# A layout of its own for the edge blocks of a windowed attention

## The chip, the cores and the metric

The kernel runs on one core of one Trainium2 chip. The metric is the device time of one execution in microseconds. The engines of the core are TensorE (PE in the profile; its weight loads are PEld), VectorE (DVE), ScalarE (ACT), GpSimd (POOL) and SyncE (SP, which here only issues DMAs). Each engine runs its own instructions in order and waits for the others by semaphores.

## What is computed

The reference is one layer of an encoder block. An input of 256 tokens and one of 2048 tokens, each with 16 learned meta tokens put ahead, are normalized and projected (1024 to 2304 columns). The columns feed two groups: a windowed attention of 8 query heads over 2 key heads, and a convolution of width 31. Both are gated, concatenated, projected back and added to the input. The part that the change is about, cut from the reference:

```python
qb = qr.reshape(B, nb, BLOCK, N_KV_HEADS, GQA_GROUP, hd)      # blocks of 128 queries
kw = jnp.concatenate([kp[:, :-2], kp[:, 1:-1], kp[:, 2:]], axis=2)   # left, own, right block of keys
valid = (jnp.abs(rel) <= WINDOW)[None] & in_range[:, None, :]
s_win = jnp.einsum('bnqkgd,bnskd->bnkgqs', qb, kw) * scale - (slopes * dist)
s_win = jnp.where(valid, s_win, -jnp.inf)
s_meta = jnp.einsum('bnqkgd,bmkd->bnkgqm', qb, km) * scale
p = softmax(concatenate([sink_b, s_meta, s_win]))
o = p_meta @ vm + p_win @ vw
```

A query sees the 16 meta keys, and the real keys at most 128 away. A sequence's first block has no left neighbour and its last block no right one.

## The kernel before

**Stages.** The input projections run first, over 18 blocks of 128 tokens in six groups of three, as three passes of products of high and low parts (each operand is split into a rounded part and its remainder). Queries, keys, values and gates go through DRAM. The convolution runs on VectorE beside the projections. During the last q projections the attention begins (`spread`, `attention_open`), and `attention_rest` runs the rest of it together with the output projection.

**Blocks and layout.** Blocks 0 and 1 are the short sequence, 2 to 17 the long one: 0 and 2 are first blocks, 1 and 17 last ones, and block 1 is followed by block 2. For each block and key head (`kv`) the scores of four query heads are made in four steps `n` of 32 queries x 4 heads = 128 rows. The key tile `kw` (two of them in turn) has 416 columns: half of the left block (`LA`), the meta keys (`MA`), the own block (`CC`), the other half of the left block (`LB`), half of the right block (`RA`), the meta keys again (`MB`), and the other half of the right block (`RB`). So each step reads one stretch of columns (`SPANS`, L62) that holds its window and the meta keys once. `span` (L312) cuts it for edge blocks; what lies in it and is not the block's (`masked`, L320) is filled with 1e30 on VectorE (L437).

**From scores to output.** `scores` (L410) issues two matmuls into a PSUM tile S (L427 in the code; the profile puts them on the wrapper's line L383), then `bias_max` (bias and row minimum, VectorE), `expo` (ScalarE) and, after the fourth step, `norm` (the reciprocal on VectorE and four products on GpSimd, L466). `bank` (L481) transposes the normalized rows in three groups: `c` the own block, `m` the columns `LB` to `MB`, `x` the meta keys with the outer half of a neighbour. Each group is four transposes into one PSUM tile, then split into high and low (`ptiles`). `pv` (L508) multiplies with the values: one matmul of 512 columns for each of high and low in `c` and `m` (L517), and in `x` two halves of 256 columns (L523), as two of the four steps need the left neighbour and two the right one. The rows of these products are 128 in `c`, 128 or 64 in `m`, 80 or 16 in `x`, with 64 and 16 where a neighbour is missing. `merge` (L532) adds the two parts, multiplies with the gate on GpSimd (L550) and splits the result for the output projection (`rest`, L554, L555).

**Order.** `slot_step` (L614) is one slot, eight to a block: one `bank` of the block before (`PLAN`, L475), two pieces of the output projection (L598, three matmuls each), one `scores` of the present block, loads, and `tick`. `later(k, f)` runs `f` at the k-th tick from there. On GpSimd the order is the program's during the attention, and from `attention_rest` on TensorE's too; for the other engines a planner sets the order from a simulated time line. The output projection of a block starts at slot 6 of the next step with the convolution's half (e = 4 to 7), and needs the attention's half (`rest`) four slots later for key head 0 and six later for key head 1.

**Loads.** `load_k` (L285) and `load_v` (L296) issue up to five and seven DMAs for a block, fewer for an edge block. `kw` holds its meta keys all the time; `km`, their source, is loaded in the middle of the projections (L1148).

Of the kernel before, what the change touches and what calls it, by code (L numbers as in the profile page):

```python
# [18 lines left out]
P = 128  # L19
# [39 lines left out]
SW = 2 * P + NM + QB  # L59
# [3 lines left out]
BOFF = (0, SW, 2 * SW, 3 * SW, 4 * SW + QB)  # L63
# [23 lines left out]
def hymba_kernel(  # L87
# [29 lines left out]
    vec = const.tile([P, 26], F32, name="vec")  # L117
# [4 lines left out]
    snk, nsnk = vec[:, 22:24], vec[:, 24:26]  # L122
# [114 lines left out]
    vt, qt, q2t, sbt, gat, gct, cnt, mix, att, yot, opj = ({} for _ in range(11))  # L237
# [3 lines left out]
    def attention_open():  # L241

        phase[0] = 2
        right_pools.close()
        man = ExitStack()
        cst['man'] = man
        man.enter_context(tc.manual_schedule(engines=MAN1))
        ap = att_pools.enter_context(tc.tile_pool(name="ap", bufs=2, side="right", reuse_waits="tile"))
        pool["a"] = ap
        cst["bias"] = bias = ap.tile([P, KV, BOFF[4]], BF16, tag="bias", name="bias", bufs=1)  # L250
        load_q(0)
        for i in range(2):
            kw.append(ap.tile([P, 2, KV, KW], F32R, tag=f"kw{i}", name=f"kw{i}", bufs=1))
        load_k(0)
        nc.sync.dma_start(bias, bias_c)
        for t, c0 in zip(kw, (LB, RA)):
            for at in (MA, MB):
                nc.gpsimd.tensor_copy(t[:, :, :, at : at + NM], km)
            nc.gpsimd.memset(t[:, :, :, c0 : c0 + QC].bitcast(F32), 0.0)
        for i in range(3):  # L260
            t = ap.tile([P, 4, KW], F32, tag=f"sb{i}", name=f"sb{i}", bufs=1)
            for n, c0 in enumerate((RA + QB, LA, RB + QB)):
                nc.vector.memset(t[:, n, c0 : c0 + QB], 0.0)
            sbs.append(t)
        load_v(0)
# [11 lines left out]
    def has_left(b):  # L277
        return b not in (0, NB_P)

    def has_right(b):  # L280
        return b not in (NB_P - 1, NB - 1)

    vt, qt, q2t, sbt, gat, gct, cnt, mix, att, yot, opj = ({} for _ in range(11))

    def load_k(b):  # L285
        t = kw[b % 2].bitcast(F32)
        at = P * (b - 1)
        nc.sync.dma_start(t[:, :, :, CC:LB], kd[:, :, :, at + P : at + 2 * P])
        if has_left(b):
            nc.sync.dma_start(t[:, :, :, LA:MA], kd[:, :, :, at : at + QC])  # L290
            nc.sync.dma_start(t[:, :, :, LB:RA], kd[:, :, :, at + QC : at + P])
        if has_right(b):
            nc.sync.dma_start(t[:, :, :, RA:MB], kd[:, :, :, at + 2 * P : at + 2 * P + QC])
            nc.sync.dma_start(t[:, :, :, RB:KW], kd[:, :, :, at + 2 * P + QC : at + 3 * P])

    def load_v(b):  # L296
        vt[b] = [
            pool["a"].tile([P, KV, P], F32R, tag=f"v{k}", name=f"v{k}_{b}", bufs=VBUFS) for k in ("c", "m", "a", "b")
        ]
        c, m, a, z_ = (t.rearrange("p a e -> p (a e)").bitcast(F32) for t in vt[b])  # L300
        nc.sync.dma_start(c, vd[b])
        r = QC if has_left(b) else 0
        if has_left(b):
            nc.sync.dma_start(m[0:QC], vd[b - 1, QC:P])
            nc.sync.dma_start(a[0:QC], vd[b - 1, 0:QC])
        nc.sync.dma_start(a[r : r + NM], vmd)
        nc.sync.dma_start(z_[0:NM], vmd)
        if has_right(b):
            nc.sync.dma_start(m[r : r + QC], vd[b + 1, 0:QC])
            nc.sync.dma_start(z_[NM:XR], vd[b + 1, QC:P])  # L310

    def span(b, n):  # L312
        c0, c1 = SPANS[n]
        if not has_left(b):
            c0 = max(c0, MA)
        if not has_right(b):
            c1 = min(c1, RA if n < 2 else RB)
        return c0, c1

    def masked(b, n):  # L320
        if not has_left(b):
            return LB
        if n >= 2 and not has_right(b):
            return RA
        return None
# [84 lines left out]
    def scores(b, kv, n):  # L410

        c0, c1 = span(b, n)
# [21 lines left out]
        def bias_max():  # L434
            off = masked(b, n)
            if off is not None:
                nc.vector.memset(ps[:, off - c0 : off - c0 + QC], BIG)  # L437
            nc.vector.tensor_tensor_reduce(  # L438
                out=sb[:, n, c0:c1],
                in0=ps[:, 0:w],  # L440
                in1=cst["bias"][:, kv, BOFF[n] + c0 - SPANS[n][0] : BOFF[n] + c1 - SPANS[n][0]],
                scale=1.0,
                scalar=nsnk[:, kv : kv + 1],
                op0=ALU.add,
                op1=ALU.min,
                accum_out=nm[:, n : n + 1],
            )
# [13 lines left out]
        def norm():  # L461
            nc.vector.tensor_tensor(es, es, rs, op=ALU.add)
            nc.vector.reciprocal(es, es)  # L463
            for k in range(4):
                a0, a1 = span(b, k)
                nc.gpsimd.tensor_scalar(  # L466
                    sb[:, k, a0:a1], sb[:, k, a0:a1], es[:, k : k + 1], 1.0, op0=ALU.mult, op1=ALU.mult
                )
# [9 lines left out]
    def edges(b):  # L478
        return (XR if has_left(b) else NM, XR if has_right(b) else NM)

    def bank(b, k, kv):  # L481
        pt = psum.tile([P, 4, P], F32, tag="b", name=f"pT{b}_{k}_{kv}")
        sb = sbt[b, kv]
        rows = [P] * 4
        for n in range(4):
            if k == "c":
                src = sb[:, n, CC:LB]
            elif k == "m":
                src = sb[:, n, LB if has_left(b) else RA : MB if has_right(b) else RA]
                rows[n] = src.shape[-1]  # L490
            else:
                r = rows[n] = edges(b)[n // 2]
                src = sb[:, n, MB : MB + r] if n >= 2 else sb[:, n, CC - r : CC]
            nc.tensor.transpose(pt[: rows[n], n, :], src, ident)  # L494

        def split():
            ph, pl = (pt_part(2 * (n_bank[0] % 4) + i) for i in range(2))
            n_bank[0] += 1
            halves = ((0, 4, rows[0]),) if rows[0] == rows[3] else ((0, 2, rows[0]), (2, 4, rows[3]))
            for n0, n1, r in halves:  # L500
                nc.scalar.copy(ph[:r, n0:n1], pt[:r, n0:n1])
                nc.vector.tensor_tensor(pl[:r, n0:n1], pt[:r, n0:n1], ph[:r, n0:n1], op=ALU.subtract)
            pv_st[b, k, kv] = (ph, pl)

        later(1, split)
        later(2, lambda: pv(b, k, kv))

    def pv(b, k, kv):  # L508
        parts = pv_st[b, k, kv]
        tc_, tm, ta, tb = vt[b]  # L510
        if k == "c":
            opj[b, kv] = psum.tile([P, 4, P], F32, tag="c", name=f"O{b}_{kv}")
        o = opj[b, kv]
        if k != "x":
            r = P if k == "c" or (has_left(b) and has_right(b)) else QC
            for i, t in enumerate(parts):
                nc.tensor.matmul(  # L517
                    o, (tc_ if k == "c" else tm)[:r, kv, :], t[:r], start=(k == "c" and i == 0), stop=False
                )
            return  # L520
        for h, (t, r) in enumerate(zip((ta, tb), edges(b))):
            for i, p in enumerate(parts):
                nc.tensor.matmul(  # L523
                    o[:, 2 * h : 2 * h + 2],
                    t[:r, kv, :],
                    p[:r, 2 * h : 2 * h + 2],
                    start=False,
                    stop=(h == 1 and i == 1),
                )
        later(1, lambda: merge(b, kv))  # L530
# [159 lines left out]
    if True:  # L690
# [424 lines left out]
        nc.sync.dma_start(vec[:, 0:24], vecs)  # L1115
# [128 lines left out]
def layout(inputs):  # L1244
# [27 lines left out]
    bias_c = np.zeros((P, KV, BOFF[4]), np.float32)  # L1272
    for kv in range(KV):
        for n in range(4):
            col = np.arange(*SPANS[n])
            seg = np.searchsorted([MA, CC, LB, RA, MB, RB], col, side="right")
            key = col - np.array([P, 0, CC, RA, RA - P, 0, RA - P + NM])[seg]
            meta = (seg == 1) | (seg == 5)
            dist = np.abs(key[None, :] - (QB * n + row % QB)[:, None]).astype(np.float32)
            full = np.where(dist <= P, slopes[4 * kv + local][:, None] * dist, np.float32(BIG))  # L1280
            bias_c[:, kv, BOFF[n] : BOFF[n + 1]] = np.where(meta[None, :], np.float32(0.0), full)
    w_out = f["w_out"][0].reshape(8, P, D)
    vecs = np.concatenate([vecs, sink], axis=1)
# [20 lines left out]
```

## Time and profile before

| | |
|---|---|
| time, median of 3 (range) | 957.39 us (957.22 to 957.50) |
| the profiled execution | 957.63 us |
| its span in the profile | 955.9 us |
| VectorE busy, instructions | 757.8 us (79%), 1295 |
| ScalarE busy, instructions | 429.0 us (45%), 1168 |
| GpSimd busy, instructions | 286.8 us (30%), 450 |
| DMA, read and written | 111.77 and 62.70 MB |

The span runs from the first to the last recorded instruction. The prediction below shows lines of several views. In the chain of waits in order of time a line is the start, the time until the next piece starts, the engine, the tile written, the line of the code, and how many instructions are merged. In the groups by line and shape it is: line, engine, operation, tile written and tiles read, sizes (rows*columns of the weights and partitions x elements streamed, for TensorE), the number, then total busy us and mean ns of one, then the idle time just before them and who ended it. The windows give busy time for each engine, then TensorE's granted clock, the DMA share and GB/s. The attention's slots begin at 578 us of the span, `attention_rest` at about 608, and the last block's values are multiplied at 926 to 944.

### The profile page before, as it was taken

To read this page: it belongs to the slowest core of one execution; us is meant where nothing else is said; L and a number is where in the kernel's file an instruction comes from. 1 tells how busy PE (TensorE), PEld (TensorE's weight loads), DVE (VectorE), ACT (ScalarE), POOL (GpSimd) and SP (SyncE) were. 2 spreads that over 40 slices of the span, in tenths; PEclk is the share of its full clock that TensorE was granted. 3 is DMA by queue.
4 is the path that set the end of the run, shared out by engine and by line. 5 is a ranking of instruction groups with operands and counts; after the bars stand their busy time and mean duration, and the time that the engine had idled before them with its cause. 6 is when DMAs were issued, how large, how long until landed. Compare 5 with 4: busy or idle time off the path is not lost.

```text
span 955.9 us, 16841 instructions
## 1 busy us (share of the span) xinstructions
PE 949.3 (99%) x5861; PEld 893.3 (93%) x5861; DVE 757.8 (79%) x1295; ACT 429.0 (45%) x1168; POOL 286.8 (30%) x450
## 2 busy tenths in 40 slices
PE   8999999999999999999999999999999999999998
PEld 8999999999999999999999999878888888888886
DVE  5579999997977789999995656777877677767763
ACT  7432111353458740011112456655666666656651
POOL 4310000283479300000001455443433242424240
PEclk9999999999999999999999999999999999999999
DMA  8585345784656593233334688965666566655411
GB/s 306 163 263 200 132 174 182 251 297 168 202 169 194 195 318 133 89 121 130 138 134 144 184 269 286 349 175 145 185 195 170 153 176 187 180 153 168 142 60 66
DMA packets 152948, 175.58 MB, mean 184 GB/s; under 512 B 44992, under 2 KB 115472, under 8 KB 152864
## 3 DMA queue, kind: packets, MB, share of 16 engines
q1 hardware_dynamic: 152864, 174.51, 56.3%
q8 instruction: 46, 0.75, 0.3%
q14 instruction: 38, 0.31, 0.1%
HBM read 111.77 MB, written 62.70 MB: 183 GB/s over the span
## 4 chain that ended last, share of the span: by engine, by line
PE 95%; DVE 2%; DMA 1%; issue 1%; POOL 0%; ACT 0%; SPq 0%; DVEq 0%; ACTq 0%
PE pj L852 42%; PE y L598 21%; PE pj L868 14%; PE S L383 4%; PE O L517 4%; PE O L523 2%; PE pT_c L494 2%; PE pT_x L494 2%; PE pT_m L494 2%; PE qT L383 1%; PE lnt L207 1%; PE lnu L226 1%; DVE y L935 1%; DMA kd<-ks 1%; DMA xn<-in_z 0%
## 5 line engine op out<-in xcount | busy, mean ns | idle before, releaser
L852 PE MATMUL pj<-xh,ws 128*128 128x384 f32 (+1 forms) x1536 | 395.9, 338 | 0.1
L935 DVE SCALAR_TENSOR_TENSOR y<-us,cw,y 128x1167 f32<-128x1167 f32 x240 | 329.3, 1438 | 0.4
L852 PEld LDWEIGHTS pj<-xh,ws 128*128 128x128 f32 x1536 | 280.1, 188 | 0.4 <-ACT xh L1105 0.4
L852 PE MATMUL pj<-xl,ws 128*128 128x384 f32 (+1 forms) x768 | 260.8, 340 | 0.1
L598 PE MATMUL y<-wo,rest 128*128 128x512 f32 (+1 forms) x672 | 173.4, 395 | 0.0
L868 PE MATMUL pj<-ws,xh 128*128 128x256 f32 (+1 forms) x880 | 165.8, 284 | 0.4 <-DVE qs L999 0.2
L852 PEld LDWEIGHTS pj<-xl,ws 128*128 128x128 f32 x768 | 144.1, 188 | 0.5 <-DVE xl L790 0.4
L598 PEld LDWEIGHTS y<-wo,rest 128*128 128x128 f32 x672 | 117.0, 189 | 22.5 <-issue 1.8
L868 PEld LDWEIGHTS pj<-ws,xh 128*128 128x128 f32 (+1 forms) x880 | 136.6, 187 | 1.4 <-issue 0.4
L868 PE MATMUL pj<-ws,xl 128*128 128x256 f32 (+1 forms) x440 | 124.1, 282 | 0.0
L450 ACT ACTIVATE sb<-sb,nm 128x304 f32<-128x304 f32 (+3 forms) x144 | 79.2, 550 | 48.2 <-DVE nm L438 47.6
L438 DVE CUSTOM_DVE_ANT_0 sb<-S,bias,vec 128x304 f32<-128x304 f32 (+3 forms) x144 | 76.2, 529 | 28.9 <-PE S L383 26.1
L960 ACT ACTIVATE go<-pj 128x384 f32<-128x384 f32 x48 | 23.5, 490 | 151.3 <-PE pj L852 138.7
L550 POOL TENSOR_TENSOR at<-at,ga 128x256 f32<-128x256 f32 x36 | 26.4, 735 | 201.8 <-DVE at L544 130.8
L466 POOL TENSOR_SCALAR sb<-sb,es 128x304 f32<-128x304 f32 (+3 forms) x144 | 75.9, 544 | 26.5 <-DVE es L463 20.6
L868 PEld LDWEIGHTS pj<-ws,xl 128*128 128x128 f32 (+1 forms) x440 | 82.2, 187 | 0.2
L134 POOL TENSOR_SCALAR ssk<-ssk 128x2 f32<-128x2 f32 x18 | 7.5, 419 | 213.2 <-ACT sqk L974 211.2
L383 PE MATMUL S<-kw,q 128*128 128x304 f32 (+3 forms) x288 | 64.1, 304 | 0.0
L383 PEld LDWEIGHTS S<-kw,q 128*128 128x128 f32 x288 | 53.1, 188 | 11.0 <-issue 0.2
L134 POOL TENSOR_SCALAR ssq<-ssq 128x4 f32<-128x4 f32 (+2 forms) x55 | 26.7, 485 | 92.8 <-ACT xn L715 74.1
L895 ACT ACTIVATE sg<-pj 128x384 f32<-128x384 f32 (+1 forms) x24 | 11.8, 493 | 82.6 <-PE pj L852 73.8
L598 PE MATMUL y<-wo,mch 128*128 128x512 f32 x144 | 47.3, 410 | 0.0
(134 smaller groups left out, 1325.9 us busy)
## 6 DMA issues: line engine op xcount, KB each, us to landing
wd<-ws SPq DMA_DIRECT2D x36, 512.0 KB, 6.1
ws<-wd SPq DMA_DIRECT2D x36, 512.0 KB, 5.7
wraw<-in_w_in SPq DMA_DIRECT2D x52, 256.0 KB, 6.4
xn<-in_z SPq DMA_DIRECT2D x18, 512.0 KB, 5.5
gd<-go SPq DMA_DIRECT2D x48, 192.0 KB, 2.1
yo<-in_z SPq DMA_DIRECT2D x36, 256.0 KB, 3.2
out_y<-yo SPq DMA_DIRECT2D x35, 256.0 KB, 2.4
kw<-kd SPq DMA_DIRECT2D x64, 128.0 KB, 3.8
```

Of the source, the lines that this page charges most:

```text
L134: nc.gpsimd.tensor_scalar(src, src, scale, eps, op0=ALU.mult, op1=ALU.add)
L383: r = f(*a, **k)
L438: nc.vector.tensor_tensor_reduce(out=sb[:, n, c0:c1], in0=ps[:, 0:w], in1=cst["bias"][:, kv, BOFF[n] + c0 - SPANS[n][0] : BOFF[n] + c1 - S ...
L450: nc.scalar.activation(sb[:, n, c0:c1], sb[:, n, c0:c1], AF.Exp, bias=nm[:, n : n + 1], scale=-1.0, accum_out=rs[:, n : n + 1],)
L466: nc.gpsimd.tensor_scalar(sb[:, k, a0:a1], sb[:, k, a0:a1], es[:, k : k + 1], 1.0, op0=ALU.mult, op1=ALU.mult)
L494: nc.tensor.transpose(pt[: rows[n], n, :], src, ident)
L517: nc.tensor.matmul(o, (tc_ if k == "c" else tm)[:r, kv, :], t[:r], start=(k == "c" and i == 0), stop=False)
L550: nc.gpsimd.tensor_tensor(at[:, pr, :], at[:, pr, :], gat[b][:, pr, :], op=ALU.mult)
L598: nc.tensor.matmul(ps, mh[mi][:, e % 4, :], wo[e, wi][:, cols], start=(e == 4 and k == 0), stop=(e == 3 and k == 2),)
L852: nc.tensor.matmul(ps[:, :n], ws[:, d, wi, P * half_i : P * half_i + P], x[xi][:, d, o : o + n], start=(k == 0), stop=(k == 3 * ND - 1),)
L868: nc.tensor.matmul(ps[:rows, :UW], x[xi][:, d, o : o + rows], ws[:, d, wi, :], start=(k == 0), stop=(k == 3 * ND - 1),)
L935: nc.vector.scalar_tensor_tensor(y[:, yo + o0 : yo + o1], u[:, o0 + k : o1 + k], cw[:, j, k : k + 1], y[:, yo + o0 : yo + o1], op0=ALU.mul ...
```

## The change

First and last blocks get a layout in which two full key blocks lie side by side: columns `CC` to `MB` hold 256 keys loaded by one DMA, with the meta keys ahead of them (first) or behind them (last). Spans hold only keys that the block has, so the fill with 1e30 goes, and the bias table gets rows for each kind. Columns of the score tile that a narrower span leaves are filled with zeros on GpSimd, as the transposes read them. The products with values take two full tiles of 128 keys in `c` and `m`.

The meta keys' part is taken apart: `norm` writes the 16 normalized meta columns of the four steps twice into a tile `pm` (128 x 128, one buffer), which one transpose turns. ScalarE copies it rounded, VectorE puts the remainder in the lower half of the rows, GpSimd spreads it by a 0/1 mask `msk` over 512 columns (`ph`), and one matmul multiplies it with `vm`, the meta values eight times over (loaded once by eight DMAs). This product comes three ticks after its transpose instead of two. Inner blocks are computed as before.

```diff
-SPANS = ((LA, RA + QB), (LA + QB, MB), (CC, RB + QB), (CC, KW))
+SPANS = {
+    "in": ((LA, RA + QB), (LA + QB, MB), (CC, RB + QB), (CC, KW)),
+    "first": tuple((MA, LB + QB * (n + 1)) for n in range(4)),
+    "last": tuple((CC + QB * n, RB) for n in range(4)),
+}
...
+    vm = const.tile([P, KV, P], F32R, name="vm")
...
-        for t, c0 in zip(kw, (LB, RA)):
+        for t in kw:
             for at in (MA, MB):
                 nc.gpsimd.tensor_copy(t[:, :, :, at : at + NM], km)
-            nc.gpsimd.memset(t[:, :, :, c0 : c0 + QC].bitcast(F32), 0.0)
...
     def load_k(b):
+        if kind(b) != "in":
+            at += P * (kind(b) == "first")
+            nc.sync.dma_start(t[:, :, :, CC:MB], kd[:, :, :, at : at + 2 * P])
+            return
...
     def load_v(b):
+        if kind(b) != "in":
+            at = b - (kind(b) == "last")
+            for k in range(2):
+                nc.sync.dma_start(t[k], vd[at + k])
+            return
...
         def bias_max():
-            off = masked(b, n)
-            if off is not None:
-                nc.vector.memset(ps[:, off - c0 : off - c0 + QC], BIG)
+            at = BIAS_AT[kind(b), n]
+            z0, z1 = {"in": (0, 0), "first": (c1, MB), "last": (CC, c0)}[kind(b)]
+            if n == 0 and b == NB_P + 1:
+                z0, z1 = c1, MB
+            if z1 > z0:
+                nc.gpsimd.memset(sb[:, n, z0:z1], 0.0)
...
         def norm():
             nc.vector.tensor_tensor(es, es, rs, op=ALU.add)
             nc.vector.reciprocal(es, es)
+            if kind(b) != "in":
+                pm = pool["a"].tile([P, 2, 4, NM], F32, tag="pm", name=f"pm{b}_{kv}", bufs=1)
+                at = MA if kind(b) == "first" else MB
+                nc.gpsimd.tensor_tensor(
+                    pm,
+                    sb[:, :, at : at + NM].unsqueeze(1).to_broadcast([P, 2, 4, NM]),
+                    es.unsqueeze(1).unsqueeze(3).to_broadcast([P, 2, 4, NM]),
+                    op=ALU.mult,
+                )
+                pmt[b, kv] = pm
...
     def bank(b, k, kv):
+        inner = kind(b) == "in"
+        if k == "x" and not inner:
+            nc.tensor.transpose(pt[:, 0, :], pmt[b, kv].rearrange("p a h m -> p (a h m)"), ident)
+        else:
+            for n in range(4):
+                c0, c1 = {"c": (CC, LB), "m": (LB, MB), "x": (LA, CC) if n < 2 else (MB, KW)}[k]
+                nc.tensor.transpose(pt[: c1 - c0, n, :], sbt[b, kv][:, n, c0:c1], ident)
...
+            if k == "x" and not inner:
+                nc.scalar.copy(pl[:, 0], pt[:, 0])
+                nc.vector.tensor_tensor(pl[64:128, 0], pt[64:128, 0], pl[64:128, 0], op=ALU.subtract)
+                nc.gpsimd.tensor_tensor(
+                    ph,
+                    pl[:, 0:1].to_broadcast([P, 4, P]),
+                    msk.unsqueeze(2).to_broadcast([P, 4, P]),
+                    op=ALU.mult,
+                )
...
-        later(2, lambda: pv(b, k, kv))
+        later(3 if k == "x" and not inner else 2, lambda: pv(b, k, kv))
...
     def pv(b, k, kv):
+        if k != "x":
+            work = [(vt[b][k == "m"], p, P, 0, 4) for p in (ph, pl)]
+        elif kind(b) == "in":
+            work = [(vt[b][2 + h], p, XR, 2 * h, 2 * h + 2) for h in range(2) for p in (ph, pl)]
+        else:
+            work = [(vm, ph, P, 0, 4)]
...
                 nc.sync.dma_start(km.bitcast(F32), kmd)
+                for r0 in range(0, P, NM):
+                    nc.sync.dma_start(vm[r0 : r0 + NM].rearrange("p a e -> p (a e)").bitcast(F32), vmd)
```

More of the change, by code (lines that the diff above doesn't have):

```diff
@@ L275, in mixing_open, with kind @@
         cst["pt"] = pt.rearrange("p a b n -> p (a b n)").rearrange("p (i n) -> p i n", n=512)
[L277 to L283, printed above, removed]
+    def kind(b):
+        return "first" if b in (0, NB_P) else "last" if b in (NB_P - 1, NB - 1) else "in"
+    vt, qt, q2t, sbt, pmt, gat, gct, cnt, mix, att, yot, opj = ({} for _ in range(12))
     def load_k(b):
@@ L301, in load_v @@
[L301 to L325, printed above, removed]
+            pool["a"].tile([P, KV, P], F32R, tag=f"v{k}", name=f"v{k}_{b}", bufs=VBUFS)
+            for k in ("c", "m", "a", "b")[: 4 if kind(b) == "in" else 2]
+        ]
+        t = [x.rearrange("p a e -> p (a e)").bitcast(F32) for x in vt[b]]
+        if kind(b) != "in":
[3 more added lines that the diff above has]
+            return
@@ L410, in scores @@
     def scores(b, kv, n):
-        c0, c1 = span(b, n)
+        c0, c1 = SPANS[kind(b)][n]
         w = c1 - c0
@@ L440, in bias_max @@
                 in0=ps[:, 0:w],
[L441 removed]
+                in1=cst["bias"][:, kv, at + c0 : at + c1],
                 scale=1.0,
@@ L498, in split @@
             n_bank[0] += 1
[L499 to L502, printed above, removed]
+            if k == "x" and not inner:
[8 more added lines that the diff above has]
+            else:
+                r = XR if k == "x" else P
+                nc.scalar.copy(ph[:r], pt[:r])
+                nc.vector.tensor_tensor(pl[:r], pt[:r], ph[:r], op=ALU.subtract)
@@ L521, in pv @@
[L521 to L530, printed above, removed]
+            work = [(vt[b][k == "m"], p, P, 0, 4) for p in (ph, pl)]
+        elif kind(b) == "in":
+            work = [(vt[b][2 + h], p, XR, 2 * h, 2 * h + 2) for h in range(2) for p in (ph, pl)]
+        else:
+            work = [(vm, ph, P, 0, 4)]
@@ L532, in merge @@
+        for i, (t, p, r, n0, n1) in enumerate(work):
+            nc.tensor.matmul(
+                opj[b, kv][:, n0:n1],
+                t[:r, kv, :],
+                p[:r, n0:n1],
+                start=(k == "c" and i == 0),
+                stop=(k == "x" and i == len(work) - 1),
+            )
+        if k == "x":
+            later(1, lambda: merge(b, kv))
     def merge(b, kv):
```

91 lines of the change are left out of this document (42 added, 49 removed).

## The prediction

> **What bounds the kernel now.** I read the page first: the span, the busy engines, and the chain of work that ended last.
>
> ```profile
> span 955.9 us, 16841 instructions
> PE 949.3 (99%) x5861; PEld 893.3 (93%) x5861; DVE 757.8 (79%) x1295; ACT 429.0 (45%) x1168; POOL 286.8 (30%) x450
> PE 95%; DVE 2%; DMA 1%; issue 1%; POOL 0%; ACT 0%; SPq 0%; DVEq 0%; ACTq 0%
> ```
>
> TensorE is the bound twice over: it is busy 949.3 of 955.9 us, and the chain runs through it for 95%. The missing 6.6 us are mostly the first loads and the last store, which the change doesn't touch. A busy TensorE is not one at its peak, though, so I went on to the chain in order of time, which gives each run of matmuls its start and the time until the next starts. First an inner block, from the meta/edge transposes (`pT_x`) to the next block's first transposes:
>
> ```profile
> 700.26 0.44 PE pT_x L494 x4
> 700.69 1.38 PE y L598 x6
> 702.07 0.28 PE S L383 x2
> 702.35 0.47 PE O L517 x2
> 702.82 1.39 PE y L598 x6
> 704.21 0.30 PE S L383 x2
> 704.52 0.48 PE O L523 x4
> 704.99 0.44 PE pT_c L494 x4
> ```
>
> Then the same eight pieces while block 2 is multiplied with its values (the first block of the long sequence), and the four that matter of block 17 (the last one):
>
> ```profile
> 640.95 0.44 PE pT_x L494 x4
> 641.39 1.39 PE y L598 x6
> 642.78 0.28 PE S L383 x2
> 643.06 0.66 PE O L517 x2
> 643.72 1.58 PE y L598 x6
> 645.30 0.31 PE S L383 x2
> 645.61 0.86 PE O L523 x4
> 646.48 0.44 PE pT_c L494 x4
> ```
>
> ```profile
> 931.82 0.66 PE O L517 x2
> 932.48 1.58 PE y L598 x6
> 934.06 0.66 PE O L523 x4
> 934.73 0.59 PE pT_c L494 x4
> ```
>
> The last six pieces take 0.28 + 0.47 + 1.39 + 0.30 + 0.48 + 0.44 = 3.36 us in the inner block and 0.28 + 0.66 + 1.58 + 0.31 + 0.86 + 0.44 = 4.13 us in block 2, though they hold the same matmuls with the same or fewer rows: 0.77 us are lost. In block 17 the four pieces take 3.49 us against 0.47 + 1.39 + 0.48 + 0.44 = 2.78: 0.71 lost. What these blocks have and the inner ones don't is seen when the groups are kept apart by shape:
>
> ```profile
> L517 PE MATMUL O<-ptiles,vm 64*128 64x512 f32 x16 | 6.1, 451 | 0.0
> L523 PE MATMUL O<-ptiles,va 16*128 16x256 f32 x8 | 2.0, 327 | 0.0
> L523 PE MATMUL O<-ptiles,vb 16*128 16x256 f32 x8 | 2.0, 325 | 0.0
> L494 PE MATMUL pT_x<-ident,sb 128*16 128x128 f32 x16 | 3.1, 272 | 0.0
> ```
>
> Products over 64 and over 16 rows exist only here: 8 pairs of each (four blocks, two key heads). A run of them costs about 0.2 us more than its columns do, and what follows it (y 1.58 for 1.39, pT_c 0.59 for 0.44) pays as well. Products over 80 rows, which inner blocks have too, pay nothing (0.48).
>
> **The change part by part**, on TensorE's own sequence. The profiled execution took 957.63 us, 1.7 us more than its span, against a median of 957.39: I subtract from the median.
>
> 1. Both key tiles are now full, so all products over 64 and 16 rows become products over 128. The 0.77 and 0.71 us go, once for each of 8 pairs of block and key head: 8 x 0.74 = 5.9 us.
> 2. The meta/edge transposes: four (0.44) become one (0.11). 8 x 0.33 = 2.6 us.
> 3. The meta/edge product: four matmuls of 256 columns (0.48) become one of 512 over 128 rows; two of those take 0.47, so one takes 0.23. 8 x 0.25 = 2.0 us.
> 4. Narrower scores. Block 0 has the widths 240 and 336 at its first and its last score:
>
> ```profile
> 578.39 0.23 PE S L383 x2
> 584.21 0.32 PE S L383 x2
> ```
>
>    A pair grows by 0.09 us over 96 columns, 0.47 ns for a column of one matmul. In a first block all four widths fall by 64 (240, 272, 304, 336 to 176, 208, 240, 272): 4 x 2 x 64 x 0.47 = 0.24 us. In a last block two fall, by 64 and 96: 0.15 us. Two blocks of each kind with two key heads: 4 x 0.24 + 4 x 0.15 = 1.6 us. No row is narrower than 240. If narrower ones stay at 0.23 us a pair, widths 176 and 208 lose 0.06 + 0.03 us eight times, 0.7 in all, and 0.9 is left. I take 1.5, since the line is straight as far as rows go, and keep 0.9.
>
>    [...]
>
> Sum on TensorE: 5.9 + 2.6 + 2.0 + 1.5 = 12.0 us.
>
> What else is removed costs nothing now and gives nothing: VectorE's fills of masked scores, shorter biases, exponentials and splits, and some twenty small key and value loads (three key loads of an edge block become one, five value loads two). VectorE and ScalarE work beside TensorE throughout; the chain has none of it. If that cover were gone they would still only have less to do.
>
> **What is added, and what hides it.** The rows:
>
> ```profile
> L568 POOL TENSOR_TENSOR cn<-cn,gc 128x512 f32<-128x512 f32 x18 | 23.2, 1286 | 0.0
> L550 POOL TENSOR_TENSOR at<-at,ga 128x256 f32<-128x256 f32 x36 | 26.4, 735 | 201.8 <-DVE at L544 130.8 <-issue 70.9
> L466 POOL TENSOR_SCALAR sb<-sb,es 128x272 f32<-128x272 f32 x16 | 8.5, 534 | 6.7 <-ACT es L459 5.9 <-DVE es L463 0.8
> L554 ACT CAST rest<-at 128x256 fp32r<-128x256 f32 x36 | 14.6, 406 | 13.6 <-POOL at L550 13.6
> L555 DVE TENSOR_TENSOR rest<-at,rest 128x256 fp32r<-128x256 f32 x36 | 18.0, 500 | 1.3 <-ACT rest L554 1.3
> ```
>
> GpSimd gets per pair a product of 128 elements (`pm`; by the 735 and 1286 ns for 256 and 512, about 0.46 us), one of 512 (`ph`, about 1.3 us), and some 26 short fills in all. Its order is the program's. Two waits come with that.
>
> The masked product: `ph` must be there before TensorE reaches the meta product, which the change puts one slot later (three ticks instead of two). Two slots of about 2.2 us lie between; the copy, the remainder and 1.3 us of GpSimd fit if GpSimd is free.
>
> The single buffer of `pm`: `norm` of key head 1 runs one slot before the transpose that reads key head 0's `pm`, so GpSimd stands until TensorE reaches that transpose. Queued behind it are the four normalizing products of that head, then (since `merge` is now a slot later, it comes after `norm`) the gate product `at*ga` of the block before, whose split the output projection needs two slots on. GpSimd to ScalarE from that transpose: 0.46 + 4 x 0.53 + 0.74 + 0.41 = 3.7 us, and four hand-overs, which I put at 0.1 us: 4.1; VectorE's remainder, needed by the third matmul only, 0.5 later. TensorE from the same transpose, in block 2's rows with the gains put in: 0.11 + 1.39 + 0.28 + 0.47 + 1.39 + 0.31 + 0.44 = 4.4 us. So it just fits. It is this tight only where two edge blocks follow each other (0 then 1, 1 then 2), at the second key head. Bounds: nothing, or 1.5 us at each of the two places if ScalarE or VectorE are busy with something else; I take 0.4 for both.
>
> DMA:
>
> ```profile
> 558.03 0.43 SPq L306 DMA_DIRECT2D va<-vmd  x1
> bias<-in_bias_c SPq DMA_DIRECT2D x1, 624.0 KB, 6.7
> ```
>
> Eight loads of the meta values (16 KB each) occupy SP for about 8 x 0.43 = 3.4 us in the middle of the projections, where nothing but the next weights, two units ahead, is behind them. The bias table grows from 1248 to 3040 columns, 624 to 1520 KB: by its own 6.7 us it lands about 10 us later, around 572; the first scores end at 578.6. Both nothing; if the table were late, the first scores would wait a few us, but projections stand between them and fill the gap. Twenty fewer issues at 0.4 to 0.6 us give SP back more than it pays.
>
> So 957.4 - 12.0 + 0.4 = **945.8 us**.
>
> **Rivals.**
> - *The narrow scores don't get cheaper* (a floor at today's narrowest pair): part 4 gives 0.9 instead of 1.5, **946.5**. For it: no row below 240 columns. Against: the straight line. [...]
> - *The lost 0.7 us are not from the row counts but from the place*, and stay: only parts 2 to 4, 957.4 - 6.1 + 0.4 = **951.7**. The first three edge blocks fall where the DMAs are busiest:
>
> ```profile
> 610.00:620.00 10.00, 10.00 (x56) 8.14 (x55) 7.89 (x25) 7.42 (x21) 2.62 (x5) 1.00 1.07 365
> 930.00:945.00 15.00, 15.00 (x77) 11.30 (x76) 5.96 (x13) 4.11 (x9) 1.33 (x3) 1.00 0.20 72
> ```
>
>   Against it: block 17 loses the same at a DMA share of 0.20 (next to last column), and the clock (before it) is 1.00 in both.
> - *The wait moves to GpSimd*: the chain above is late by 1 to 2 us wherever `pm` or `ph` is used early, 3 to 6 us in all: **948.5 to 951.5**. For it: one buffer, program order, 0.3 us to spare.
> - *TensorE is freed and waits all the same*, for VectorE at 79% or a load: **957**. Against: the chain shows no such wait in any slot, and these slots lose VectorE work too.
> - *Slower*: the `pm` chain misses not twice but in all eight pairs, because `ph` of the meta product stands behind it too and TensorE, in program order, stops at that product. It decides from 12.0 / 8 = 1.5 us lost in each pair; at 2.5 us it gives 957.4 - 12.0 + 8 x 2.5 = **965**. For `ph` this needs GpSimd to be 1.5 us behind at a point two slots after the transpose, with 0.46 + 2.1 + 0.74 + 1.3 = 4.6 us of work ahead of it and about 6 us of slots: against.
>
> **How the numbers follow.** Forecast 0.52, floor 0.20, stays with the place 0.07, GpSimd 0.14, no change 0.03, slower 0.04. The likeliest time is 945.8. Below, stretches fully gone without a stall give 945.4, and some 1.6 us more for the uneven groups of block 0, which lie between projection matmuls and are harder to read: 943.8. Above, I reach to 951.7, which takes in the floor, the place and most of the GpSimd cases. 0.2% (1.9 us) is about what a measurement of this kernel can tell from no change. Faster by more: 0.52 + 0.20 + 0.07 + 0.14 = 0.93; within: 0.03; slower: 0.04.
>
> **What would show it.** In the profile after: no products over 64 or 16 rows, and y pieces of 1.39 and O pieces of 0.47 in all blocks (part 1); one pT_x of 0.11 in eight places (part 2); one O at L523's place of 0.23 (part 3); score pairs of 0.17 and 0.20, or of 0.21 to 0.23 (part 4); and TensorE waiting for GpSimd's `ptiles` or for `rest` in the first two edge blocks, if anywhere. I am wrong if y pieces of 1.58 stay without short products, or if waits of TensorE for GpSimd or ScalarE come to more than 1 us.

## The result, and the profile after

| | before | changed |
|---|---|---|
| time, median (range), first comparison | 957.44 us (957.22 to 957.81, 4 runs) | 947.34 us (947.32 to 951.75, 4 runs) |
| time, second comparison | 957.20 us (957.08 to 959.0, 7 runs) | 948.41 us (947.21 to 949.40, 4 runs) |
| ratio to before, 95% interval | | 0.9906 (0.9877 to 0.9934); 0.9905 (0.9890 to 0.9919) |
| the profiled execution, its span | 957.63, 955.9 us | 947.32, 945.3 us |

The change makes the kernel about 1% faster: 10.1 us in the first comparison, 8.8 in the second. The page after, in the lines that answer to those of before:

```profile
span 945.3 us, 16681 instructions
PE 938.1 (99%) x5813; PEld 887.7 (94%) x5813; DVE 748.8 (79%) x1263; ACT 424.1 (45%) x1160; POOL 296.7 (31%) x490
PE 85%; DMA 5%; DVE 4%; SPq 2%; POOL 1%; ACT 1%; issue 1%; DVEq 0%; POOLq 0%; ACTq 0%
```

TensorE has 48 instructions less, is busy 11.2 us less, and still for 99% of the span. But the chain that ended last is TensorE's for 85% only, where it was 95%: somewhere it now leaves TensorE for other engines and for DMAs. (The share tells where the chain runs, not how long TensorE stands; that is 1.19 us, below.) Both halves of the story are in these lines, the gain in the second and a loss in the third.

First the gain. The chain in order of time, while block 2 is multiplied with its values (start, time to the next piece, what):

```profile
640.03 1.39 PE y L609 x6
641.42 0.28 PE S L383 x2
641.70 0.23 PE O L533
...
644.49 0.11 PE pT_x L495
644.60 1.38 PE y L609 x6
```

The meta transposes are one piece of 0.11, the meta product one of 0.23, and `y` takes 1.39 as in an inner block, where it took 1.58 here before. Block 17 says the same: its `y` pieces take 1.38 to 1.40, its `O` pairs 0.47. The narrow scores of block 17, and what follows them:

```profile
906.33 0.21 PE S L383 x2
...
908.40 0.19 PE S L383 x2
908.59 0.51 PE O L533 x4
```

The last pairs are 208 and 176 columns wide. By their columns they would take 0.20 and 0.17. The pair at 908.40 shows 0.19, but the O behind it takes 0.51 instead of 0.48: the pair costs 0.22 in all, whatever is narrower.

Now the loss. TensorE's waits between 560 and 640 us, in the matmuls and in their weight loads (who waited for whom: us in all, times, longest):

```profile
PE pj L879 <- ACT sqq L980: 0.5, 1, 0.5
...
PEld y L609 <- DVE rest L566: 0.3, 1, 0.3
```

Laid out by the starts of the matmuls, these are three gaps: 0.31 us in front of the first scores (580.2), 0.78 in front of the last projection of q (604.0), 0.10 in front of an output product of block 0 (622.4): 1.19 us. ScalarE's own sequence shows what the first two come from (last bracket: idle before, and what ended it):

```profile
576.16 0.37 ACT L1004 COPY qr<-pj 128x256 f32<-128x256 f32 x1 [4.36 <-DMA qd<-qr]
...
604.05 0.37 ACT L1004 COPY qr<-pj 128x256 f32<-128x256 f32 x1 [2.94 <-DMA qd<-qr]
```

ScalarE copies q out of PSUM into a buffer whose old content hasn't been stored yet. Behind the copy stand the split of q for the first scores, and the squares that free a projection's bank. The profile before shows no wait of ScalarE for a store of q. And it is SyncE's queue that issues the stores late:

```profile
569.95 0.59 SPq L322 DMA_DIRECT2D va<-vd  x1
570.58 1.20 SPq L323 DMA_DIRECT2D va<-vmd  x1
...
572.29 0.52 SPq L325 DMA_DIRECT2D vb<-vd  x1
...
573.84 0.33 SPq L195 DMA_DIRECT2D qd<-qr  x1
```

These `va`, `vb` belong to blocks 3 and 4, far ahead. First and last blocks no longer use those tiles, so the tiles are free, and the planner puts the loads here, in front of the stores of q (experiment 4 tests it). GpSimd's new groups, at last (busy, mean ns | idle before, what ended it):

```profile
L507 POOL TENSOR_TENSOR ptiles<-ptiles,vec 128x512 fp32r<-128x512 f32 x8 | 8.3, 1041 | 1.3 <-DVE ptiles L506 1.3
L470 POOL TENSOR_TENSOR pm<-sb,es 128x128 f32<-128x128 f32 x8 | 3.2, 400 | 22.9 <-PE pT_x L495 12.0 <-DVE es L466 6.1 <-DVE at L555 3.7
```

GpSimd does stand 12 us for the transposes that free `pm`, as the forecast said it would. Whether that costs anything can't be read from this profile, since TensorE's gaps name ScalarE.

### The profile page after: what moved, and what is told of

The parts are those of the page before. It is cut to its first block, busy times and chain, and to the rows that moved or that the text cites. A ratio compares the mean times of both kernels' runs of the same rounds, so it can differ in the third digit from the quotient of the medians.

```text
span 945.3 us, 16681 instructions
## 1 busy us (share of the span) xinstructions
PE 938.1 (99%) x5813; PEld 887.7 (94%) x5813; DVE 748.8 (79%) x1263; ACT 424.1 (45%) x1160; POOL 296.7 (31%) x490
## 4 chain that ended last, share of the span: by engine, by line
PE 85%; DMA 5%; DVE 4%; SPq 2%; POOL 1%; ACT 1%; issue 1%; DVEq 0%; POOLq 0%; ACTq 0%
PE pj L863 41%; PE y L609 21%; PE pj L879 8%; PE O L533 5%; PE S L383 4%; PE pT_c L499 2%; PE pT_m L499 2%; PE pT_x L499 1%; DMA kw<-kd 1%; DMA qd<-qr 1%; DVE xt L772 1%; DVE y L946 1%; PE qT L383 1%; DMA cd<-zn 1%; DMA wraw<-in_w_in 1%
## 5 line engine op out<-in xcount | busy, mean ns | idle before, releaser
L441 DVE CUSTOM_DVE_ANT_0 sb<-S,bias,vec 128x304 f32<-128x304 f32 (+5 forms) x144 | 74.4, 517 | 32.2 <-PE S L383 31.4
L453 ACT ACTIVATE sb<-sb,nm 128x304 f32<-128x304 f32 (+5 forms) x144 | 77.8, 541 | 48.9 <-DVE nm L441 48.2
L479 POOL TENSOR_SCALAR sb<-sb,es 128x304 f32<-128x304 f32 (+5 forms) x144 | 73.1, 526 | 16.0 <-DVE es L466 13.2
L383 PEld LDWEIGHTS S<-kw,q 128*128 128x128 f32 x288 | 53.2, 188 | 11.3 <-issue 0.3
L383 PE MATMUL S<-kw,q 128*128 128x304 f32 (+5 forms) x288 | 62.7, 299 | 0.2 <-issue 0.2
```

The lines of the kernel that those rows point to most:

```text
L383: r = f(*a, **k)
L441: nc.vector.tensor_tensor_reduce(out=sb[:, n, c0:c1], in0=ps[:, 0:w], in1=cst["bias"][:, kv, at + c0 : at + c1], scale=1.0, scalar=nsnk[:, ...
L453: nc.scalar.activation(sb[:, n, c0:c1], sb[:, n, c0:c1], AF.Exp, bias=nm[:, n : n + 1], scale=-1.0, accum_out=rs[:, n : n + 1],)
L479: nc.gpsimd.tensor_scalar(sb[:, k, a0:a1], sb[:, k, a0:a1], es[:, k : k + 1], 1.0, op0=ALU.mult, op1=ALU.mult)
```

## The experiments

Every kernel is the changed one with the edit shown; ratios are to the kernel before, measured beside it.

**1. Are the row counts the cause of the 0.77 us?** Put the short product back, alone:

```diff
-            work = [(vm, ph, P, 0, 4)]
+            work = [(vm, ph, 64, 0, 4)]
```

> The changed kernel, with the meta product of the eight edge pairs over the first 64 of its 128 rows; the remainders of the meta probabilities, in the other 64 rows, are left out of the product. Nothing else differs. Theory (products over few rows cost time of their own, before, in and behind them): each of the eight products brings back about 0.3 us (in the profile of before a product over 64 rows starts 0.09 us late, takes 0.10 more, and what follows starts 0.11 late), 2.4 us in all: 949.7 against 947.3. Rival (the stretches came from the place, not from the rows): 947.3, within 0.3.

Measured 951.17 (950.53 to 952.86), ratio 0.9938 (0.9923 to 0.9952). With 80 rows in the same place:

> As e1_rows64, but over the first 80 rows (three quarters of the remainders are left out). Theory, by the inner blocks' products over 80 rows, which pay nothing: 947.3, within 0.3, and no piece of the chain longer than in the changed kernel. A rival in which fewer rows than 128 cost by themselves: 949.7 here too.

Measured 948.65 (947.87 to 950.24), ratio 0.9911 (0.9896 to 0.9925). The difference, 2.5 us for eight products, is 0.31 each. Both kernels lie about 1.4 us above what was expected, so the expectation of 947.3 for 80 rows missed: TensorE waits 1.1 and 1.2 us for `sqq` in them, 0.5 in the changed kernel. So the rows of the chain are the better witness. Block 2 of the first kernel:

```profile
643.12 0.28 PE S L383 x2
643.40 0.43 PE O L533
643.83 0.59 PE pT_m L499 x4
```

One product over 64 rows takes 0.43 for 0.23, and the transposes behind it 0.59 for 0.44. That is 0.35 us in the rows. Same place, same queues: it is the row count, not the place. At 80 rows no row pays (0.23 and 0.44 at the same place).

**2. Is there a floor under the scores?** No span of an edge block narrower than 240:

```diff
-    "first": tuple((MA, LB + QB * (n + 1)) for n in range(4)),
-    "last": tuple((CC + QB * n, RB) for n in range(4)),
+    "first": tuple((MA, LB + QB * max(n + 1, 3)) for n in range(4)),
+    "last": tuple((CC + QB * min(n, 1), RB) for n in range(4)),
```

> The changed kernel with no score of an edge block narrower than 240 columns: 176 and 208 are widened to 240 by keys that the bias table shuts out (1e30), so the result is the same. Theory (a matmul of scores never takes less than 0.112 us, so 176 and 208 columns already cost what 240 do): TensorE's pieces stay, 947.3 within 0.4. Rival (time goes with the columns, 0.47 ns each, as predicted): 0.09 us for each of eight pairs, 948.0.

Measured 949.74 (949.02 to 951.09), ratio 0.9922 (0.9906 to 0.9939). The same stretch of block 17, the pairs 240 wide:

```profile
908.64 0.22 PE S L383 x2
...
910.72 0.22 PE S L383 x2
910.94 0.48 PE O L533 x4
```

0.22 + 0.48 is the 0.19 + 0.51 of the narrow pair: 176 columns save nothing against 240. The time is longer all the same, by gaps at 573, 580, 605 and 624 (0.2, 1.5, 1.4 and 0.3 us by the starts of the matmuls), the last three the same waits for `q`, `sqq` and `rest` as in the changed kernel, only larger. They come to 3.5 us here and 1.2 in the changed kernel, and the spans of the two profiles differ by the same 2.3 us (947.6 and 945.3). So it is these gaps, not TensorE's work, that make this kernel slower.

**3. A floor of what?** Groups of 16 products behind the end of the kernel:

> The changed kernel with 21 groups of 16 independent products added behind its end, back to back, 4-byte operands: (1) widths 512 to 64 columns with 128 x 128 weights, (2) widths 208, 176, 112, 64 with 64 and 32 weight columns, (3) width 512 with every second product over 80, 64 or 16 rows and one group over 64 rows throughout. Some 45 us on top of 947. Theory of the floor as weight loading: in (1) the start-to-start time follows 0.441 ns a column down to about 0.112 us near 240 columns and stays there; in (2) the floor falls with the weight columns, to some 0.06 us at 64. Rival, a floor of the product itself: 0.112 us whatever the weight columns. Short rows: (128, 80) costs nothing over 0.231 us; (128, 64) and (128, 16) cost some 0.2 us per short product; (64, 64) costs nothing if it is the change between the two row counts that is paid, 0.2 us for each if it is the short product itself.

Measured 996.5. TensorE in stretches cut at the groups' starts (start:end, length, busy and count of matmuls, of weight loads, granted clock, DMA share, GB/s; the counts take in neighbours at the edges, each stretch has 16 products):

```profile
941.27:945.00 3.73, 3.73 (x16) 3.01 (x17) 1.00 0.40 141
...
949.25:951.04 1.79, 1.79 (x19) 1.79 (x17) 1.00 0.04 9
951.04:952.81 1.77, 1.77 (x18) 1.77 (x17) 1.00 0.00 0
...
958.13:959.89 1.76, 1.76 (x19) 1.76 (x18) 1.00 0.00 0
...
962.76:963.68 0.92, 0.92 (x18) 0.92 (x17) 1.00 0.00 0
963.68:964.59 0.91, 0.91 (x19) 0.91 (x18) 1.00 0.06 18
...
967.41:968.24 0.83, 0.83 (x19) 0.83 (x17) 1.00 0.00 0
968.24:968.75 0.51, 0.51 (x20) 0.51 (x18) 1.00 0.00 0
968.75:972.60 3.85, 3.85 (x22) 2.92 (x18) 1.00 0.00 0
972.60:976.52 3.92, 3.92 (x17) 2.88 (x17) 1.00 0.00 0
976.52:983.35 6.83, 6.83 (x17) 2.95 (x16) 1.00 0.01 2
```

Divide by 16. With 128 weight columns: 512 wide 0.233 us, 240 wide 0.112, 208 wide 0.111, and 64 wide still 0.110. In the narrow stretches the weight load is busy all of the time (equal second and third numbers), but that alone decides nothing: at a width of 304, above the floor, it is so too (2.23 of 2.24 us). What decides is the weight columns. With 64 of them, widths of 112 and 64 take 0.058 and 0.057 us (962.76 and 963.68), a floor of half the height; with 32 they take 0.052 and 0.032 (967.41 and 968.24), and no floor is reached. So the floor goes with the weight columns: 0.111 us with 128 of them, half of that with 64. That it is the time of the weight load is how I read this; no run takes the load apart from the rest of a product.

The last three stretches are 512 wide with every second product over 80 rows, all over 64, and 128 and 64 in turn. The first two take about 0.24 each with what their edges add (0.23 from start to start inside them); the third 0.427. A short product costs nothing among its like; the **change** between 64 and 128 rows costs 0.427 - 0.233 = 0.194 us, each time. In the kernel before, a pair had two short groups, so four changes: 4 x 0.194 = 0.78, and 0.77 had been read from block 2. What TensorE does in the 0.194 us, no run here shows. (A group that alternates 128 and 16 rows fell partly in a stretch at a granted clock of 0.59; its first four products took 0.43.)

**4. Are the early loads the cause of the gaps?** Hold the inner blocks' loads in the program's order:

```diff
+    def held(dst, src):
+        tc.keep_in_program_order(nc.sync.dma_start(dst, src))
...
-        nc.sync.dma_start(t[0], vd[b])
+        held(t[0], vd[b])
```

(and so for all twelve loads of `load_k` and `load_v` of an inner block; the lines below are 3 higher for it.)

> The changed kernel with the key and value loads of inner blocks held in program order on SP, so that those of blocks 3 and 4 are no longer issued between 563 and 573 us of the span, ahead of the stores of q. Theory (these early loads delay the stores qd<-qr; ScalarE waits for them, and behind it TensorE stands 0.3 us before the first score and 0.7 us before the last projection): ScalarE's wait for qd<-qr goes from 7.3 us to under 1, both stalls go, 946.3. Rival (the stores are late because the bias table and the output weights fill the DMA engines): the waits and stalls stay, 947.3.

Measured 947.57 (947.52 to 947.62), ratio 0.9897 (0.9882 to 0.9912). Half a miss. ScalarE's waits for the store of q fall from 7.3 us to 1.1, both gaps go, and four runs agree to 0.1 us where those of the changed kernel lie 2 to 4 us apart. But the time doesn't fall, for a new gap stands at 607. The chain of this kernel, and VectorE and GpSimd in their own sequence:

```profile
603.20 1.43 DVE qr L1013
...
607.81 0.61 DVE ptiles L519
...
608.46 0.74 PE O L536 x2
```

```profile
603.12 1.51 DVE L1013 TENSOR_TENSOR qr<-qr,rqq 128x256 f32<-128x256 f32 x1
```

```profile
599.41 0.40 POOL L473 TENSOR_TENSOR pm<-sb,es 128x128 f32<-128x128 f32 x1 [4.87 <-issue]
599.91 1.74 POOL L482 TENSOR_SCALAR sb<-sb,es 128x176 f32<-128x176 f32 x4
...
603.06 1.29 POOL L582 TENSOR_TENSOR cn<-cn,gc 128x512 f32<-128x512 f32 x1
604.31 1.22 POOL L510 TENSOR_TENSOR ptiles<-ptiles,vec 128x512 fp32r<-128x512 f32 x1
```

Two things stand out. GpSimd idles 4.87 us in front of `pm` of block 0's second key head, and everything behind it comes late and in a bunch. The profile names no releaser for this idle time; the transpose that reads the buffer starts at 599.16, just before, and with a second buffer (experiment 6) the idle time is 0.00. And VectorE's scaling of q, 0.43 us elsewhere, takes 1.51 beside GpSimd's `cn`.

**5. The buffer of `pm`, alone, beside the changed kernel again and beside more buffers for q.** The edits are `bufs=2` for `pm`, and `bufs=6` instead of 3 for the pool that holds the q pieces.

> The changed kernel itself once more, as the yardstick of its neighbours on the same chip: 947.3 us in most runs and up to 951.8 in some, if the spread of the first runs (947.32, 951.75, 947.32, 947.36) belongs to the kernel; 947.3 in all, if the odd run was the chip's.

Measured 948.41 (947.21 to 949.40): the spread shows again, so it is not one chip's. But a part of it is not the change's either. In some executions the first product of the projections starts about 0.9 us later: at 12.31 us in the profile of the first comparison (947.32), at 13.13 in this one (947.97). From the start of that product to the end of the last output product the two take 929.87 and 929.74 us, the kernel before 940.10. Why the start moves, no run here shows. I use this stretch below, as it leaves the start out.

> A second buffer for the scaled meta probabilities (pm), so that the product of the second key head no longer waits for the transpose of the first. Theory from the changed kernel's trace: the 12 us for which GpSimd stood before L470 are gone and TensorE gains the 0.1 us that it stood at 622.4 behind the first output product of the next block: 947.2. Rival (the wait I priced at 0.4 us in the forecast, here allowed to be more, since what GpSimd does late also decides when ScalarE and VectorE get to the q pieces): 946.3 or less.

Measured 948.38 (947.92 to 950.41), ratio 0.9909 (0.9894 to 0.9924). GpSimd's 12 us are gone, the gap at 622 is gone, and nothing is gained (930.09 us from the first product on): gaps at 574 and 605 (0.65 and 0.6 us) are in their place, with one wait of ScalarE for a store of 4.8 us still there. Both expected times missed.

> Six buffers instead of three for the q pieces that ScalarE copies out of the last projection (and the gate pieces of the same pool), nothing else. Theory: ScalarE's 7.3 us of waiting for stores of q go, and with them the TensorE gaps at 580.2 (0.31) and 604.0 (0.78); runs agree with each other to 0.3 us, since the landing of a DMA no longer sets the order: 946.2. Rival: the gaps come of the order in which the planner put ScalarE's work, the stores being only the last to arrive; then another wait ends there (the scale factor from GpSimd or the projection's bank) and the time stays at 947.0 to 947.6.

Measured 947.35 (946.75 to 947.99), ratio 0.9893 (0.9876 to 0.9909). ScalarE's waits for the store fall to 0.9 us, but others end there:

```profile
PE O L533 <- DVE ptiles L516: 0.4, 1, 0.4
PE lnu L240 <- DVE zn L234: 0.3, 1, 0.3
```

The first is the gap of the held kernel, the second another buffer that waits for its store (VectorE's `zn`, 6.6 us for `cd<-zn`). Against the changed kernel measured beside it, it is inconclusive: the ranges overlap. The runs agree to 1.2 us, not to the 0.3 expected.

**6. Both at once.** If the late stores and the single buffer each hold up the same stretch, taking one away shows nothing.

> The kernel with the inner blocks' loads held in program order (its own time 947.57, its last stall 1.3 us in front of the output products at 606.8), and the product of the convolution half (cn) of block 0 issued one slot earlier. Theory: VectorE's products with two operands in SBUF do not run while GpSimd's product of two tensors runs (the scaling of q, L1013, took 1.51 us at 603.12 beside cn's 1.29 us, where 13 others took 0.41 to 0.43), and that lateness is the stall at 606.8. Moved away, cn leaves its place to the product for the meta keys (L510, 1.22 us), which would then stand beside the same scaling: it still takes over 1 us, and the time falls by 0.5 us at most: 947.1 to 947.6. Rival (the load on VectorE and ScalarE there is too much whoever holds whom): the scaling returns to 0.43 us and the stall stays at 1.0 us or more.

Measured 947.63 (947.60 to 948.65), ratio 0.9900 (0.9885 to 0.9915). This one tells nothing apart: `cn` is issued earlier, but GpSimd stands in front of it as before, so it ran at 604.02, beside the scaling of q again (1.47 us).

> Held loads and a second buffer for pm. GpSimd no longer stands from 594.5 to 599.4, so its scaling of the probabilities and the meta product come up to 5 us earlier, and the cn product, now at about 601.5 to 603, may only touch the scaling of q. Theory of the held VectorE: the scaling of q falls from 1.51 us to 1.0 or less, the stall at 606.8 falls by as much (0.5 us or more), and that at 622 (0.1 us, VectorE's remainder of the merged heads took 0.89 us beside GpSimd's meta product) goes: 946.3 to 947.2. Rival: the stall stays and the time with it, 947.5.

Measured 946.51 (945.93 to 946.94), ratio 0.9884 (0.9867 to 0.9900).

> All three: held loads, second pm buffer, cn of block 0 one slot earlier. Theory of the held VectorE: nothing of GpSimd with two tensors stands beside the scaling of q near 603, it takes 0.43 us, the stall at 606.8 falls under 0.4 us: 945.6 to 946.6, the fastest of all variants. Rival: 947.5 as the held kernel alone.

Measured 946.17 (945.91 to 946.24), ratio 0.9881 (0.9867 to 0.9896). Against the held kernel with `cn` moved (947.63), the kernel with both takes 1.1 us less by the medians, and the one with all three 1.5; no run of theirs overlaps a run of that one. The late start blurs this. From the first product on, the profiles give:

| | us | first product at |
|---|---|---|
| before | 940.10 | 12.33 |
| changed, and again | 929.87, 929.74 | 12.31, 13.13 |
| second buffer alone | 930.09 | 13.25 |
| loads held; with `cn` moved | 930.10, 930.16 | 12.28, 13.25 |
| loads held and second buffer | 928.59 | 13.22 |
| all three | 928.62 | 12.15 |

So the second buffer gains 1.5 us once the loads are held, and nothing without; moving `cn` gains nothing in either case. In the last two TensorE shows no wait between 560 and 640 us. The chain of the first of these is TensorE's throughout:

```profile
608.07 0.47 PE O L536 x2
608.54 0.11 PE pT_x L498
608.65 1.39 PE y L612 x6
```

The expectation for all three missed in its mechanism, though the time came in: the scaling of q still meets `cn` and takes 1.51 us (at 598.09), where without the move of `cn` it takes 0.42 (at 599.13; there `cn`, begun with it, takes 1.57 for 1.29), and neither kernel has a gap. So a VectorE held by GpSimd doesn't by itself cost the kernel time here.

**7. What holds VectorE?** Sixteen products of VectorE beside GpSimd, behind the end of the kernel:

> The changed kernel with five groups of 16 VectorE products (128x256, 4-byte) added behind its end, the first with GpSimd idle, the others beside 8 GpSimd operations (128x512): (1) both operands in SBUF, alone; (2) the same beside GpSimd products of two tensors; (3) the same beside GpSimd scalings of one tensor; (4) one operand in PSUM, beside products of two tensors; (5) one operand in PSUM, beside scalings. Some 50 us on top. Theory of the held VectorE: (1) 0.42 us each; (2) single ones of 1.2 to 1.7 us, each ending after a GpSimd product has ended; (3) about 0.64 us where one meets the end of a scaling, as the remainders of the merged heads take beside L479; (4) and (5) 0.42 us throughout. Rival (memory or instruction order, not what the operands share): (2) and (4) take the same.

Measured 999.81. VectorE's and GpSimd's sequences:

```profile
946.77 7.31 DVE L709 TENSOR_TENSOR pdcn<-pdga,pdgc 128x256 f32<-128x256 f32 x16
954.13 14.84 DVE L709 TENSOR_TENSOR pdcn<-pdga,pdgc 128x256 f32<-128x256 f32 x16
969.03 9.62 DVE L709 TENSOR_TENSOR pdcn<-pdga,pdgc 128x256 f32<-128x256 f32 x16
978.70 7.29 DVE L709 TENSOR_TENSOR pdcn<-pps,pdgc 128x256 f32<-128x256 f32 x16
...
989.70 7.29 DVE L709 TENSOR_TENSOR pdcn<-pps,pdgc 128x256 f32<-128x256 f32 x16
```

```profile
954.30 11.18 POOL L705 TENSOR_TENSOR pgcn<-pgga,pggc 128x512 f32<-128x512 f32 x8 [17.14 <-DVE pgga L710]
969.20 5.95 POOL L707 TENSOR_SCALAR pgcn<-pgga 128x512 f32<-128x512 f32 x8 [3.73 <-DVE pgga L710]
```

Alone 16 take 7.31 us; beside products of two tensors 14.84, beside scalings 9.62. Eight of them meet a GpSimd instruction and take 1.37 or 0.71 us, each ending 0.28 us after it, while GpSimd's own product grows only from 1.26 to 1.32. With one operand in PSUM nothing is lost (7.29 both times). The rival falls: beside the same products of GpSimd it is 14.84 with both operands in SBUF and 7.29 with one in PSUM. What VectorE and GpSimd share there, no run here shows.

## Why the prediction held, and which steps did not

The forecast was 945.8, the range 943.8 to 951.7; measured 947.3 and 948.4. The gain on TensorE was understood; the waits were not. Step by step:

1. **Products over 64 and 16 rows**, 5.9 us: right. The pieces are the inner blocks' now, experiment 1 excludes the place as a cause, and the probe of experiment 3 gives what is paid, four changes of 0.194 us in each pair.
2. **One meta transpose** (0.11, 2.6 us) and **one meta product** (0.23, 2.0 us): right, to the rows.
3. **Narrower scores**, 1.5 us: mis-sized. The straight line of the rows ends at 240 columns, below which a pair takes 0.22. With that floor, in a first block only the widths 272, 304 and 336 gain (to 0.22, 0.22 and 0.25: 0.03 + 0.06 + 0.05 us), in a last block two pairs by 0.03 each: 4 x 0.14 + 4 x 0.06 = 0.8 us. The rival "floor" was true, and its own 0.9 a little too high (its time, by its own sum, is 946.4 and not 946.5). The prediction names pairs of 0.21 to 0.23 us as the sign of a floor; no row of before stands for the 0.21 (240 columns take 0.22 to 0.23 there), and the runs showed 0.22.
4. **Added waits**, 0.4 us: wrong in place and too small. Where I put them (`rest` in front of the output product, blocks 0 to 1 and 1 to 2) there is 0.10 us at one place. With the loads held, the same single buffer costs 1.5 us earlier, at block 0's second key head, where GpSimd's work for the projections stands behind `pm`; I had followed that queue only into the output projection.
5. **DMAs moved, "nothing"**: wrong. I had looked at what stands behind the added loads, not at what the planner would do with tiles that edge blocks no longer need. Loads for blocks 3 and 4 went in front of the stores of q, and ScalarE waited for these.

The prediction also named its sign of being wrong: waits of TensorE for GpSimd or ScalarE of more than 1 us. By the starts of the matmuls, the two gaps behind ScalarE's late copies come to 0.31 + 0.78 = 1.09 us. So by its own sign its account of the waits failed, while the time fell inside the range. The two errors have the same sign, 0.7 us in step 3 and 0.8 in the waits (1.19 for 0.4), and 945.8 + 0.7 + 0.8 = 947.3. That the range took them in is luck in part: its upper end was there for the place and for a late GpSimd chain, and in neither profile of the changed kernel is TensorE's largest wait for GpSimd.

The sum with its true sizes: 5.9 + 2.6 + 2.0 + 0.8 = 11.3, so 957.4 - 11.3 = 946.1 with no wait at all; the last kernel of experiment 6 measures 946.17, and from the first product on it takes 940.10 - 928.62 = 11.5 us less than before. The changed kernel stands 1.2 us above that one in the same stretch, and its three gaps come to 1.19. Steps 4 and 5 are not to be added. Removing either alone changed no median by more than the runs of the kernel differ (947.57 and 948.38 against 947.3 to 948.4); removing both gave 946.5 and less. That the two waits hold up the same stretch of ScalarE, VectorE and GpSimd is how I read this; no single wait was followed through all three. What stays open is how much of the buffer's 1.5 us is GpSimd's own lateness, and how much the order that the planner gives VectorE and ScalarE behind it.

## What to carry to other kernels

Read a piece of a chain against the same piece in a block without the oddity: the 0.77 us found so agree with four changes of 0.194, and came from changes of the row count, not from short rows as such. A straight line through rows is good only between them; look for what runs beside the thing measured (here, as I read it, the weight load) and ask where it becomes the longer of the two. And when a change frees a buffer, follow the loads that may now start early to the queue they share with stores; two waits over the same stretch hide each other, so test them together as well as one by one. Where runs of one kernel differ, take the stretch from a fixed first instruction to a fixed last one before you believe a difference of 1 us.

## What was not expected of the hardware

- A change of row count between 64 and 128 costs 0.19 us on TensorE (0.427 a product for 0.233, in the probe); between 80 and 128, nothing that shows (0.23 from start to start there).
- A VectorE product with both operands in SBUF can end after a whole GpSimd instruction that runs beside it (0.28 us after, in the probe). A product of 0.43 us takes up to 1.51; it did so in the kernel before as well, once (1.50 at 600.43, beside `cn`), with nothing waiting for it.
- Runs of the changed kernel lie up to 4.4 us apart, those of the four kernels with the loads held 0.1 to 1.1. About 0.9 us are the late start, which kernels without early loads show as well (13.25 and 13.22 us in two of the held ones). That the early loads bring the rest is argued from these few runs, not shown.
